# Moving the key-by-receptance products of a delta-rule recurrence ahead of it, through DRAM, and reordering one layer's projections

## Chip, cores, metric

One core of one Trainium2 chip runs the whole program. The metric is device time in microseconds (us) of that core. The kernel before has a median of 1447.89 us over 3 runs (1444.70 to 1640.55).

## What is computed

Two layers run over 1152 tokens (1024 of a prompt, 8 samples of 16) with 1024 features. Each layer normalises x, projects it to 24 features of 128 outputs, computes four branches from these, gates them, and projects the result back:

```python
z = rms_norm(x, p['norm_g']) @ p['w_in']
ya, shift_n, wkv_n = rwkv7_mix(za, shift0, s0, p)     # A: delta rule, per-token scan
yb, ckv, kr = mla_prompt(zb, p)                       # B: latent attention
yd, pool_n = pool_mix(zd, None, p)                    # D: trailing means of 2, 4, 8, 16 tokens
yc, vn = sgu_mix(zc, p)                               # C: spatial gating
y = jnp.concatenate([ya, yb, yc, yd], axis=-1) * jax.nn.silu(gates)
out = x + y @ p['w_out']
```

Branch A, for every token and each of 4 heads of 64, is

```python
sa = einsum('bhij,bhj->bhi', s, -kk_t)
s = s * w_t + outer(sa, kk_t * a_t) + outer(v_t, k_t)
y_t = einsum('bhij,bhj->bhi', s, r_t)
```

Branch C normalises its values over their 256 channels (`layer_norm`), mixes them over 128 positions and multiplies by u.

## The kernel before

Tokens are cut into 3 groups of 384. `project` makes one feature: 24 matmuls a group (8 slices of x, each as high by high, high by low and low by high part) into one of two PSUM buffers (`pj`), then a sink function that takes the result over. Weights come in quarter features: one DMA on SP (L238, three buffers), the high part on ACT (L241), the low part on POOL (L242), eight buffers each.

After chosen slices of a group, and after each sink, `project` calls `tick()`, which steps each open generator (a "lane") once. What TensorE does besides the projection is so laid between its matmuls, by hand, in program order. `inproj` sets the slices: (2, 5) gives 3 ticks a group, (1, 3, 5) gives 4. The order of the features is `F_ORDER`: WDAD and K0 together, K1, R0, R1, V0, V1 (keys, receptances, values of branch A), D0, GD0, D1, GD1 (pooling and its gates), VC0, VC1 (values of branch C), U0, GC0, U1, GC1 (its gating), and then attention.

Branch A works on 18 chunks of 64 tokens (16 prompt chunks, and 16 and 17 with the samples). `a_elem` (lane "a", once per key half and group) makes the decayed keys `kb` and the decayed negative keys and receptances `ar`. `systems` makes for each chunk the 64x64 products of keys (4 matmuls of 64x64 into `b`, a mask on DVE into `ns`, L514, two buffers) and writes them to DRAM (`nd`, L515, issued on ACT), two chunks per tick. `solve` loads all these systems, inverts 16x16 (samples) and 32x32 blocks with DVE alone (L538 a product, L540 an addition, 15 and 31 steps), copies (L550) and writes the inverses to DRAM (`dd`, L552 and L553, issued on ACT). `recurrence` then runs chunk by chunk, three ticks a chunk, in the order 16, 17, 0, ..., 15: `prepare` loads the inverse `tt` (L571, SP), makes the full products of keys with keys and receptances `gm` (4 matmuls of 64x128, two DVE masks of 128x256, L580), transposes keys and values (L586, L588); `advance` carries the state on.

`solve` is queued behind K1's systems, and `recurrence` is queued after D0, so that its first chunk comes in GD0. `pool_in` (D0, D1) takes windows with POOL and DVE (L784, L791). `gating` runs VC0 and VC1, then `norms` in lane "v" beside U0: for each of 9 blocks of 128 tokens two transposes on TensorE into one of two `st` PSUM buffers (L848), DVE statistics (L850, L852) and scaling (L855), two POOL operations (L856, L857), into tiles that GC0 and GC1 read.

Of the kernel before, what the change touches and what calls it, by code (L numbers as in the profile page):

```python
# [20 lines left out]
NS, SL = 8, 16  # L21
# [27 lines left out]
def tile_trunk(ctx: ExitStack, tc: tile.TileContext, *aps):  # L49
# [295 lines left out]
    for l in range(L):  # L345
# [14 lines left out]
        def inproj(f, sink):  # L360
            ticks = (3,)
            if f in (K1, R0, R1, V0, V1, D0, GD0, D1, GD1, VC0, VC1, GC0, U1, GC1,
                     GA0, GA1):
# [63 lines left out]
        def a_elem(i, g, k):  # L427
# [43 lines left out]
            V.scalar_tensor_tensor(out=kk, in0=k, scalar=vcol(V_KK + i), in1=q, op0=ALU.mult, op1=ALU.mult)  # L471
            V.scalar_tensor_tensor(out=ar[:, :, 0, :], in0=chv(kk), scalar=-1.0, in1=chv(ep),
                                   op0=ALU.mult, op1=ALU.mult)

            recip1p(av)
# [23 lines left out]


        nd, nds = halves(f"nd{l}", 32, 64), halves(f"nds{l}", 4, 64)

        def hp(h):
            return slice(64 * (h % 2), 64 * (h % 2) + 64)

        def systems(g):
            for cl in range(6):
                c = 6 * g + cl
                pn = pb()[:, 0:128].rearrange("p (i t) -> p i t", i=2)
                for h in range(4):  # L510
                    mm(pn[hp(h), h // 2, :], KB[h // 2][g][hp(h), cl, h % 2, :], AR[h // 2][g][hp(h), cl, 0, :])
                ns = chp.tile([128, 2, 64], F32, tag="u0", name=nm("ns"), bufs=2)
                mk = cm[:, C_MP if c < 16 else C_MS, 0:64]
                V.tensor_tensor(out=ns, in0=pn, in1=mk.unsqueeze(1).broadcast_to([128, 2, 64]), op=ALU.mult)  # L514
# [45 lines left out]
        def prepare(c):  # L560
# [12 lines left out]
            Gm = chp.tile([128, 2, 2, 128], F32, tag="gm", name=nm("gm"), bufs=2)  # L573
            for hh in range(2):
                pg = pb()[:, 0:256].rearrange("p (i t) -> p i t", i=2)
                pr = slice(64 * hh, 64 * hh + 64)
                for i in range(2):
                    mm(pg[:, i, :], KB[i][g][pr, cl].rearrange("p a t -> p (a t)"),
                       AR[i][g][pr, cl].rearrange("p a t -> p (a t)"))
                V.tensor_tensor(out=Gm[:, hh], in0=pg,  # L580
                                in1=cm[:, C_MS if samp else C_MP, :].unsqueeze(1).broadcast_to([128, 2, 128]),
                                op=ALU.mult)

# [241 lines left out]

        def gating():
            sg = m_tile(1024)
            sgb = sg[:, 0:512].rearrange("p (a i t) -> p a i t", a=2, i=2)
            SY.dma_start(out=sgb, in_=sgub[l])
            sgg = sg[:, 512:1024].rearrange("p (a t) -> p a t", a=2)  # L830
            SY.dma_start(out=sgg, in_=sgugb[l])
            vraw = []
            for fv in (VC0, VC1):
# [5 lines left out]
                vraw.append(vr)  # L839
            vn = [m_tile(1024), m_tile(1024), m_tile(1024)]  # L840

            def vnt(j):
                return vn[j // 4][:, (j % 4) * 256:(j % 4 + 1) * 256]

            def normalise(j):
                ps = st()[:, 0:256]
                for i in range(2):
                    PE.transpose(ps[:, i * 128:(i + 1) * 128], vraw[i][:, j * 128:(j + 1) * 128], ident)  # L848
                bs = smp.tile([128, 6], F32, tag="bs", name=nm("bs"))
                V.bn_stats(out=bs, in_=ps)  # L850
                mv = smp.tile([128, 2], F32, tag="mv", name=nm("mv"))
                V.bn_aggr(out=mv, in_=bs)  # L852
                rs = smp.tile([128, 1], F32, tag="rs1", name=nm("rs1"))
                rsqrt(rs, mv[:, 1:2], 1.0, ELN)
                V.tensor_scalar(out=vnt(j), in0=ps, scalar1=mv[:, 0:1], scalar2=rs, op0=ALU.subtract, op1=ALU.mult)  # L855
                Po.tensor_tensor(out=vnt(j), in0=vnt(j), in1=sgg[:, 0], op=ALU.mult)  # L856
                Po.tensor_tensor(out=vnt(j), in0=vnt(j), in1=sgg[:, 1], op=ALU.add)  # L857

            def norms():
                for j in range(9):  # L860
                    normalise(j)
                    if j % 2:
                        yield
                A.dma_start(out=vn_o[l], in_=vnt(8))
            go("v", norms())
            wst = m_tile(1024).rearrange("p (a h t) -> p a h t", a=2, h=4)
            SY.dma_start(out=wst[:, 0], in_=wsT[l])
# [6 lines left out]
            for i, (fu, fg) in enumerate(((U0, GC0), (U1, GC1))):  # L874
# [4 lines left out]
                inproj(fu, sink_u)  # L879
                finish("v")  # L880

# [23 lines left out]
        def after_k1(g, zs):  # L905
            start("a", a_elem(1, g, zs))
            if g > 0:
                go("a", systems(g - 1))
# [12 lines left out]
        values(V1)  # L921
        A.dma_start(out=shift_o[l], in_=sho)
        pool_in(0, D0)
        go("a", recurrence())
# [678 lines left out]
```

## Time and profile before

| | |
|---|---|
| median of 3 runs | 1447.89 us (1444.70, 1447.89, 1640.55) |
| profiled execution | 1447.32 us |
| its span, first to last instruction | 1445.5 us |
| granted TensorE clock, mean | 0.986 |
| TensorE (PE) busy | 1358.6 us, 94% of the span |
| DVE, ACT, POOL busy | 786.8, 746.6, 465.2 us |
| DMA traffic | 97.40 MB, 67 GB/s mean |

A row of a group of instructions gives the line, the engine, the operation, what it writes and reads, shapes and count; then the busy time of all, the mean of one in ns, and the idle time of the engine just ahead of them with what ended it. A matrix product of float32 data stands in the trace as several records: the 72 matmuls of 64x64 a layer are 288 records over both layers. A window row gives the busy time of each engine in a stretch of the span. A timeline row gives start, duration, engine and instruction, and in square brackets the idle time that went before on that engine. "SPq" and "ACTq" rows are DMA issues.

The layer 0 stages start at 15.4 us (WDAD and K0), 68.5 (K1), 90.7 (R0), 113.4 (R1), 131.3 (V0), 144.8 (V1), 159.3 (D0), 173.3 (GD0), 210.3 (D1), 234.0 (GD1), 261.8 (VC0), 289.9 (VC1), 314.3 (U0), 348.0 (GC0), 366.5 (U1), 379.2 (GC1) and 394.6 us (attention); those of layer 1 at 782.0 (K1), 871.3 (D0), 922.1 (D1), 1022.4 (U0) and 1055.2 us (GC0).

### The profile page before, as it was taken

Reading aid. Unit: us, or ns where it says so; the run is one execution under the profiler, and the core shown is the slowest. Engines: PE = TensorE matmul, PEld = TensorE weight load, DVE = VectorE, ACT = ScalarE, POOL = GpSimd, SP = SyncE. Lnnn points to the kernel's source line nnn. Section 1 sums busy time; section 2 is a strip of 40 time slices with the busy share of each in tenths; the row PEclk is TensorE's granted clock in tenths of the full one; section 3 lists DMA queues with packets and bytes.
Section 4 is the critical chain, followed back from the end, with each engine's and each line's share of the span. In section 5 each row is a group of like instructions: output and inputs, shape, how many; then the busy total and the mean of one; then the engine's idle time right before and its main releaser. Section 6 shows DMA issues by size and latency. Waiting matters only on the chain. (4 is left out here: it accounts for less than half of the span.)

```text
span 1445.5 us, 26910 instructions
## 1 busy us (share of the span) xinstructions
PE 1358.6 (94%) x9962; PEld 1160.2 (80%) x9962; DVE 786.8 (54%) x1766; ACT 746.6 (52%) x2013; POOL 465.2 (32%) x600
## 2 busy tenths in 40 slices
PE   4899989999999999999989998999999999899999
PEld 3768868888988886679977788788789788766998
DVE  6984954435235567742287948444532374777211
ACT  6762234655466677642257621555654676866210
POOL 4514404336411033332162234232653111322320
PEclk9799999999999999999999999999999999999999
DMA  7113241110312214033300122321022111131232
GB/s 222 52 32 75 63 102 42 61 49 25 96 46 70 60 37 128 5 116 93 99 22 30 49 64 66 92 69 49 29 71 74 52 57 59 45 103 45 74 95 77
DMA packets 116596, 97.40 MB, mean 67 GB/s; under 512 B 46129, under 2 KB 111345, under 8 KB 116465
## 3 DMA queue, kind: packets, MB, share of 16 engines
q1 hardware_dynamic: 76776, 73.74, 17.6%
q10 hardware_dynamic: 39688, 21.94, 5.1%
q8 instruction: 79, 1.29, 0.4%
q14 instruction: 53, 0.43, 0.1%
HBM read 71.48 MB, written 24.16 MB: 66 GB/s over the span
## 5 line engine op out<-in xcount | busy, mean ns | idle before, releaser
L76 PE MATMUL pj<-xh,wh 128*128 128x384 f32 x1152 | 415.4, 361 | 18.9 <-ACT xh L280 7.2
L76 PE MATMUL pj<-xl,wh 128*128 128x384 f32 x1152 | 396.4, 344 | 2.4 <-POOL xl L282 2.0
L76 PE MATMUL pj<-xh,wl 128*128 128x384 f32 x1152 | 396.3, 344 | 0.0
L242 POOL TENSOR_TENSOR wl<-wr,wh 128x256 fp32r<-128x256 f32 x200 | 157.0, 793 | 465.9 <-ACT wh L241 390.5
L76 PEld LDWEIGHTS pj<-xh,wh 128*128 128x128 f32 x1152 | 221.6, 193 | 41.7 <-ACT sho L400 11.3
L76 PEld LDWEIGHTS pj<-xl,wh 128*128 128x128 f32 x1152 | 222.1, 193 | 9.0 <-POOL xl L282 3.3
L76 PEld LDWEIGHTS pj<-xh,wl 128*128 128x128 f32 x1152 | 221.4, 192 | 6.0 <-issue 4.8
L76 PE MATMUL pj<-yh,wh 128*128 128x384 f32 x384 | 129.3, 337 | 2.4 <-DVE x L1426 2.4
L76 PE MATMUL pj<-yh,wl 128*128 128x384 f32 x384 | 128.6, 335 | 0.0
L76 PE MATMUL pj<-yl,wh 128*128 128x384 f32 x384 | 128.3, 334 | 0.0
L241 ACT ACTIVATE wh<-wr 128x256 fp32r<-128x256 f32 x200 | 81.0, 414 | 84.7 <-PE pj L76 41.0
L242 POOL TENSOR_TENSOR wl<-m,wh 128x256 fp32r<-128x256 f32 x56 | 43.7, 790 | 102.0 <-ACT wh L241 84.4
L76 PEld LDWEIGHTS pj<-yh,wh 128*128 128x128 f32 x384 | 72.1, 188 | 3.7 <-DVE x L1426 2.8
L76 PEld LDWEIGHTS pj<-yl,wh 128*128 128x128 f32 x384 | 72.1, 188 | 0.1
L76 PEld LDWEIGHTS pj<-yh,wl 128*128 128x128 f32 x384 | 72.1, 188 | 0.1
L1293 ACT ACTIVATE X<-b,ng 128x512 f32<-128x512 f32 (+3 forms) x96 | 55.0, 577 | 25.3 <-DVE ng L1285 21.4
L76 PE MATMUL b<-sp,cr 128*128 128x384 f32 (+3 forms) x192 | 59.5, 385 | 3.2 <-POOL sp L99 2.8
L1281 DVE TENSOR_REDUCE mx<-b 128x1 f32<-128x512 f32 (+3 forms) x96 | 53.0, 556 | 9.8 <-PE b L76 8.0
L1422 DVE TENSOR_TENSOR pt<-pj,pt 128x384 f32<-128x384 f32 x24 | 13.4, 557 | 80.6 <-PE pj L76 80.6
L76 PEld LDWEIGHTS st<-X,X 128*64 128x64 f32 x576 | 35.1, 136 | 27.4 <-ACT X L1311 7.6
L241 ACT ACTIVATE wh<-m 128x256 fp32r<-128x256 f32 x56 | 22.4, 413 | 61.0 <-PE pj L76 59.9
L1304 PE MATMUL pj<-cm,X 128*128 128x128 f32 x288 | 48.0, 286 | 5.0 <-ACT X L1293 5.0
(307 smaller groups left out, 2591.7 us busy)
## 6 DMA issues: line engine op xcount, KB each, us to landing
wr<-in_win_dram SPq DMA_DIRECT2D x176, 128.0 KB
m<-in_wout_dram SPq DMA_DIRECT2D x12, 512.0 KB
x<-in_xT_dram SPq DMA_DIRECT2D x12, 384.0 KB
ysp<-m ACTq DMA_DIRECT2D x24, 192.0 KB
pt<-in_xT_dram SPq DMA_DIRECT2D x24, 192.0 KB
ea<-ysp SPq DMA_DIRECT2D x24, 192.0 KB
x1d<-x ACTq DMA_DIRECT2D x24, 192.0 KB
pt<-x1d SPq DMA_DIRECT2D x24, 192.0 KB
```

Source lines behind the costliest of these rows:

```text
L76: return PE.matmul(out, lhsT=lhsT, rhs=rhs, start=start, stop=stop, skip_group_check=True)
L241: A.activation(out=h, in_=r, func=AF.Copy)
L242: Po.tensor_tensor(out=lo, in0=r, in1=h.bitcast(F32), op=ALU.subtract)
L1281: V.tensor_reduce(out=mx[:, b:b + 1], in_=pc[:, :w], axis=AX.X, op=ALU.max)
L1293: A.activation(out=P[:, :w], in_=pc[:, :w], func=AF.Exp, scale=SCALE, bias=ng, accum_out=sums[pr][:, b, s, h:h + 1])
L1304: PE.transpose(ptp[:, j * 128:(j + 1) * 128], Pb[slot][:, j * 128:(j + 1) * 128], ident)
L1422: V.tensor_tensor(out=xr, in0=ps, in1=xr, op=ALU.add)
```

## The change

The order of features becomes WDAD, K0, V0, R0, K1, R1, V1, VC0, VC1, D0, GD0, D1, GD1, U0, and on as before. `systems` makes the full products `gm` at once, one chunk per tick, from the second receptance's sink on, and stores with three SP DMAs per chunk: the key part into `nd` (two halves) and the whole tile, 256 KB, into a new DRAM tensor `gd`. `prepare` loads `gm` from `gd`. `a_elem` loses a subtraction and an exponential and uses the exponentials of the token before; one scaling moves from DVE to ACT. The gating values VC0, VC1 come ahead of the pooling, their norms run beside D0 and go to DRAM (`vnd`) and back. D1 and GD1 get 4 ticks a group in place of 3.

```diff
-F_ORDER = (WDAD, K0, K1, R0, R1, V0, V1, D0, GD0, D1, GD1, VC0, VC1, U0, GC0, U1, GC1,
+F_ORDER = (WDAD, K0, V0, R0, K1, R1, V1, VC0, VC1, D0, GD0, D1, GD1, U0, GC0, U1, GC1,
...
-            elif f in (U0, GB0, GB1):
+            elif f in (D1, GD1, U0, GB0, GB1):
                 ticks = (1, 3, 5)
...
-            V.tensor_tensor(out=rw, in0=cs, in1=rw, op=ALU.subtract)
-            ep = rw
-            A.activation(out=ep, in_=rw, func=AF.Exp, scale=-DECAY_C)
...
-            V.scalar_tensor_tensor(out=ar[:, :, 0, :], in0=chv(kk), scalar=-1.0, in1=chv(ep),
+            V.scalar_tensor_tensor(out=ar[:, :, 0, 1:], in0=chv(kk)[:, :, 1:], scalar=-1.0, in1=ex[:, :, 0:63],
                                    op0=ALU.mult, op1=ALU.mult)
+            V.tensor_scalar(out=ar[:, 0:nch, 0, 0], in0=chv(kk)[:, 0:nch, 0], scalar1=-1.0, scalar2=None, op0=ALU.mult)
...
-            V.tensor_scalar(out=av, in0=av, scalar1=vcol(V_KA + i), scalar2=nv[:, 11 + i:12 + i],
-                            op0=ALU.mult, op1=ALU.add)
+            A.activation(out=av, in_=av, func=AF.Identity, scale=vcol(V_KA + i), bias=nv[:, 11 + i:12 + i])
...
                 Po.tensor_tensor(out=ex, in0=chv(zs), in1=ex, op=ALU.mult)
+                if i == 1:
+                    go("a", systems(g))
...
-                pn = pb()[:, 0:128].rearrange("p (i t) -> p i t", i=2)
-                for h in range(4):
-                    mm(pn[hp(h), h // 2, :], KB[h // 2][g][hp(h), cl, h % 2, :], AR[h // 2][g][hp(h), cl, 0, :])
-                ns = chp.tile([128, 2, 64], F32, tag="u0", name=nm("ns"), bufs=2)
...
-                A.dma_start(out=whole(nd, c, 64) if c < 16 else whole(nds, c - 16, 64),
-                            in_=ns.rearrange("p i t -> p (i t)"))
-                if cl % 2:
-                    yield
+                Gm = chp.tile([128, 2, 2, 128], F32, tag="gm", name=nm("gm"), bufs=2)
...
+                    for i in range(2):
+                        mm(pg[:, i, :], KB[i][g][pr, cl].rearrange("p a t -> p (a t)"),
+                           AR[i][g][pr, cl].rearrange("p a t -> p (a t)"))
+                    V.tensor_tensor(out=Gm[:, hh], in0=pg, in1=mk.unsqueeze(1).broadcast_to([128, 2, 128]),
+                                    op=ALU.mult)
+                for hh in range(2):
+                    half = nds[2 * (c - 16) + hh] if samp else nd[2 * c + hh]
+                    SY.dma_start(out=half[0:128 * 64].rearrange("(s i t) -> s i t", s=64, i=2),
+                                 in_=Gm[64 * hh:64 * hh + 64, hh, :, 0:64])
+                SY.dma_start(out=gd[c], in_=Gm.rearrange("p h i t -> p (h i t)"))
+                yield
...
             Gm = chp.tile([128, 2, 2, 128], F32, tag="gm", name=nm("gm"), bufs=2)
-            for hh in range(2):
...
+            SY.dma_start(out=Gm.rearrange("p h i t -> p (h i t)"), in_=gd[c])
...
+                t = s_tile("gn", 3, 256)
+                V.tensor_scalar(out=t, in0=ps, scalar1=mv[:, 0:1], scalar2=rs, op0=ALU.subtract, op1=ALU.mult)
+                Po.tensor_tensor(out=t, in0=t, in1=sgg[:, 0], op=ALU.mult)
+                Po.tensor_tensor(out=t, in0=t, in1=sgg[:, 1], op=ALU.add)
+                SY.dma_start(out=vnd[j], in_=t)
...
+        def gating():
+            finish("v")
...
+                SY.dma_start(out=vn[a][:, 0:256 * n].rearrange("p (j t) -> p j t", j=n),
+                             in_=vnd[4 * a:4 * a + n].rearrange("j p t -> p j t"))
...
-        shifted(K1, lambda g: zk1[:, gcols(g)], after_k1)
-        go("a", idle(4))
-        go("a", systems(2))
-        go("a", idle(4))
+        values(V0)
+        receptance(0, R0)
+        shifted(K1, lambda g: zk1[:, gcols(g)], after_k1)
+        receptance(1, R1)
         go("a", solve())
-        receptance(0, R0)
-        receptance(1, R1)
-        values(V0)
         values(V1)
         A.dma_start(out=shift_o[l], in_=sho)
+        gating_values()
         pool_in(0, D0)
         go("a", recurrence())
```

DVE beside D0 of layer 0, before: solve steps (L538, L540) with the pooling windows (L791) between them.

```order
L791 SCALAR_TENSOR_TENSOR m_1717<-pt_1747,pinv_t,m_1716 64x384
L538 TENSOR_TENSOR m_1395<-m_1394,m_1393 128x252
L791 SCALAR_TENSOR_TENSOR m_1717<-pt_1749,pinv_t,m_1716 64x384
L540 TENSOR_TENSOR m_1394<-m_1394,m_1395 128x18x14
L538 TENSOR_TENSOR m_1395<-m_1394,m_1393 128x247
```

The same place now: solve steps (L551, L553), at an earlier step of the inversion, with the norms' statistics (L851, L853) and scalings (L857) between them.

```order
L553 TENSOR_TENSOR m_1706<-m_1706,m_1707 128x7x25
L851 BN_STATS bs_2012<-st_2009 128x6
L551 TENSOR_TENSOR m_1707<-m_1706,m_1705 128x192
L853 BN_AGGR mv_2014<-bs_2012 128x2
L851 BN_STATS bs_2027<-st_2024 128x6
L553 TENSOR_TENSOR m_1706<-m_1706,m_1707 128x8x24
L857 TENSOR_SCALAR gn_2019<-st_2009,mv_2014,rs_398_2016 128x256
L551 TENSOR_TENSOR m_1707<-m_1706,m_1705 128x207
```

At the first norm the block size of a solve step is 7x25 there, that is step 7 of 31, where before the pooling began at step 17; two solve operations stand between one norm's scaling and the next one's.

SP's DMA issues beside the recurrence of layer 0, before (`wr` weights, `tt` inverses, `m` tables of the gating):

```order
L571 DMA tt_2305<-dd_291 128x1x256
L829 DMA m_2937<-in_sgub_dram 128x512
L831 DMA m_2937<-in_sgugb_dram 128x512
L571 DMA tt_2414<-dd_291 128x1x256
L238 DMA wr_2524<-in_win_dram 128x256
L571 DMA tt_2558<-dd_291 128x1x256
```

and now, near the end of GD1:

```order
L584 DMA tt_2668<-dd_291 128x1x256
L587 DMA gm_2670<-gd_314 128x512
L584 DMA tt_2770<-dd_291 128x1x256
L874 DMA m_3458<-in_sgub_dram 128x512
L587 DMA gm_2772<-gd_314 128x512
L879 DMA m_3460<-vnd_318 128x4x256
L879 DMA m_3462<-vnd_318 128x4x256
L584 DMA tt_2872<-dd_291 128x1x256
```

Each chunk's load of `tt` has a load of `gm` behind it, of twice its size, and the normalised values come back through the same queue.

SP beside R1 and V1 now, where it issued weights alone before:

```order
L238 DMA wr_1566<-in_win_dram 128x256
L528 DMA nd_79_312<-gm_1296 128x1x64 x2
L530 DMA gd_314<-gm_1296 128x512
L528 DMA nd_79_312<-gm_1321 128x1x64 x2
L530 DMA gd_314<-gm_1321 128x512
L238 DMA wr_1590<-in_win_dram 128x256
```

Two chunks' six stores, each of which waits for its chunk's masks, stand between two weight loads.

## Rows read from the trace of the kernel before

**Rows 1.** The page's first part: engine, busy time, share of the span, instructions.

```profile
PE 1358.6 (94%) x9962; PEld 1160.2 (80%) x9962; DVE 786.8 (54%) x1766; ACT 746.6 (52%) x2013; POOL 465.2 (32%) x600
```

**Rows 2.** Windows: length, busy time per engine, granted clock, DMA share, GB/s.

```profile
68.50:159.30 90.80, 84.62 (x526) 72.32 (x526) 64.18 (x158) 40.24 (x105) 28.09 (x40) 0.97 0.20 54
159.30:210.30 51.00, 43.01 (x384) 38.14 (x382) 38.65 (x87) 15.99 (x50) 15.70 (x23) 0.97 0.36 77
210.30:234.00 23.70, 23.70 (x293) 20.43 (x292) 9.59 (x20) 10.68 (x41) 12.21 (x17) 1.00 0.26 83
234.00:348.00 114.00, 107.83 (x1272) 91.92 (x1271) 50.54 (x121) 62.52 (x215) 45.78 (x57) 0.99 0.16 48
366.50:379.20 12.70, 12.70 (x75) 12.61 (x74) 1.74 (x4) 4.57 (x11) 6.56 (x10) 1.00 0.50 153
782.00:871.30 89.30, 82.50 (x527) 70.70 (x527) 64.85 (x160) 41.83 (x109) 28.25 (x40) 1.00 0.21 55
871.30:922.10 50.80, 44.07 (x385) 39.10 (x383) 38.47 (x83) 15.98 (x50) 15.76 (x23) 0.93 0.34 77
922.10:1055.20 133.10, 130.05 (x1564) 111.14 (x1562) 59.54 (x140) 72.95 (x256) 57.70 (x73) 1.00 0.18 55
```

**Rows 3.** TensorE's products of `kb` and `ar`, by form, both layers.

```profile
L76 PE MATMUL b<-ar,kb 64*128 64x128 f32 x288 | 27.9, 298 | 0.0
L76 PE MATMUL b<-ar,kb 64*64 64x64 f32 x288 | 15.3, 228 | 4.6 <-DVE ns L514 3.7 <-DVE kb L481 0.8
```

**Rows 4.** Timeline, R1 of layer 0: two issues of `nd`, and a mask's wait.

```profile
121.47 0.49 ACTq L515 DMA_DIRECT2D nd<-ns  x1
...
124.65 0.29 DVE L514 TENSOR_TENSOR ns<-b,cm 128x128 f32<-128x128 f32 x1 [1.55 <-DMA nd<-ns]
```

**Rows 5.** DVE's masks and two operations of `a_elem`, by form, both layers.

```profile
L580 DVE TENSOR_TENSOR gm<-b,cm 128x256 f32<-128x256 f32 x72 | 28.3, 418 | 6.2 <-PE b L76 6.1
L514 DVE TENSOR_TENSOR ns<-b,cm 128x128 f32<-128x128 f32 x36 | 10.4, 288 | 22.5 <-DMA nd<-ns 21.1 <-PE pj L76 1.3
L463 DVE TENSOR_TENSOR ea<-ea,ea 128x384 f32<-128x384 f32 x12 | 7.8, 653 | 0.3
L482 DVE TENSOR_SCALAR ea<-ea,vcs,nv 128x384 f32<-128x384 f32 x12 | 7.4, 617 | 0.2
```

**Rows 6.** The solve on DVE, layer 0, from 143 to 188 us.

```profile
L538 DVE TENSOR_TENSOR m<-m,m 128x31 f32<-128x31 f32 (+15 forms) x31 | 13.5, 435 | 0.8
L540 DVE TENSOR_TENSOR m<-m,m 128x31 f32<-128x31 f32 (+15 forms) x31 | 13.2, 424 | 0.8
L538 DVE TENSOR_TENSOR m<-m 32x15 f32<-32x15 f32 (+7 forms) x15 | 3.8, 251 | 1.3 <-POOL wl L242 0.9
L540 DVE TENSOR_TENSOR m<-m 32x15 f32<-32x15 f32 (+7 forms) x15 | 3.5, 232 | 0.4
```

**Rows 7.** The norms of the gating values by form, both layers.

```profile
L855 DVE TENSOR_SCALAR m<-st,mv,rs 128x256 f32<-128x256 f32 x18 | 9.3, 533 | 0.7 <-ACT rs L214 0.7
L850 DVE BATCH_NORM_STATS2 bs<-st 128x6 f32<-128x256 f32 x18 | 7.1, 424 | 1.3 <-PE st L848 1.0
L848 PE MATMUL st<-cm,m 128*128 128x128 f32 x36 | 6.8, 289 | 3.6 <-DVE m L855 3.6
L856 POOL TENSOR_TENSOR m<-m,m 128x256 f32<-128x256 f32 x18 | 13.7, 762 | 4.7 <-DVE m L855 3.9 <-DVE mv L852 0.7
```

**Rows 8.** Timeline, D0 of layer 0: solve steps and a POOL operation.

```profile
160.00 0.39 DVE L540 TENSOR_TENSOR m<-m,m 128x220 f32<-128x220 f32 x1
...
160.80 0.73 POOL L242 TENSOR_TENSOR wl<-wr,wh 128x256 fp32r<-128x256 f32 x1 [1.09 <-ACT wh L241]
...
160.86 0.94 DVE L540 TENSOR_TENSOR m<-m,m 128x231 f32<-128x231 f32 x1
```

**Rows 9.** Waits of TensorE in GD0 of layer 0: us, times, longest.

```profile
PE b L76 <- DVE gm L580: 3.2, 2, 3.0
PE b L76 <- DVE m L666: 1.5, 2, 1.3
PE b L76 <- ACT m L610: 1.4, 1, 1.4
```

**Rows 10.** Timeline, GD1 of layer 0: an issue of `tt` and its first use.

```profile
230.60 0.50 SPq L571 DMA_DIRECT2D tt<-dd  x1
...
237.81 0.42 PE L76 MATMUL b<-tt,gm 64*64 64x32 f32 x8 [1.58 <-DMA tt<-dd]
```

More of the change, by code (lines that the diff above doesn't have):

```diff
@@ L361, in inproj @@
             ticks = (3,)
-            if f in (K1, R0, R1, V0, V1, D0, GD0, D1, GD1, VC0, VC1, GC0, U1, GC1,
+            if f in (K1, R0, R1, V0, V1, D0, GD0, VC0, VC1, GC0, U1, GC1,
                      GA0, GA1):
                 ticks = (2, 5)
-            elif f in (U0, GB0, GB1):
+            elif f in (D1, GD1, U0, GB0, GB1):
                 ticks = (1, 3, 5)
@@ L471, in a_elem @@
             V.scalar_tensor_tensor(out=kk, in0=k, scalar=vcol(V_KK + i), in1=q, op0=ALU.mult, op1=ALU.mult)
-            V.scalar_tensor_tensor(out=ar[:, :, 0, :], in0=chv(kk), scalar=-1.0, in1=chv(ep),
+            V.scalar_tensor_tensor(out=ar[:, :, 0, 1:], in0=chv(kk)[:, :, 1:], scalar=-1.0, in1=ex[:, :, 0:63],
                                    op0=ALU.mult, op1=ALU.mult)
+            V.tensor_scalar(out=ar[:, 0:nch, 0, 0], in0=chv(kk)[:, 0:nch, 0], scalar1=-1.0, scalar2=None, op0=ALU.mult)
+            if n < G:
+                V.tensor_scalar(out=ar[:, nch:, 0, :].rearrange("p c (s t) -> p c s t", t=SL)[:, :, :, 0],
+                                in0=chv(kk)[:, nch:].rearrange("p c (s t) -> p c s t", t=SL)[:, :, :, 0],
+                                scalar1=-1.0, scalar2=None, op0=ALU.mult)
             recip1p(av)
@@ L501, in tile_trunk @@
         nd, nds = halves(f"nd{l}", 32, 64), halves(f"nds{l}", 4, 64)
+        gd = dr.tile([18, 128, 512], F32, tag=f"gd{l}", name=nm("gd"))
         def hp(h):
@@ L508, in systems @@
                 c = 6 * g + cl
-                pn = pb()[:, 0:128].rearrange("p (i t) -> p i t", i=2)
-                for h in range(4):
-                    mm(pn[hp(h), h // 2, :], KB[h // 2][g][hp(h), cl, h % 2, :], AR[h // 2][g][hp(h), cl, 0, :])
-                ns = chp.tile([128, 2, 64], F32, tag="u0", name=nm("ns"), bufs=2)
-                mk = cm[:, C_MP if c < 16 else C_MS, 0:64]
-                V.tensor_tensor(out=ns, in0=pn, in1=mk.unsqueeze(1).broadcast_to([128, 2, 64]), op=ALU.mult)
-                A.dma_start(out=whole(nd, c, 64) if c < 16 else whole(nds, c - 16, 64),
-                            in_=ns.rearrange("p i t -> p (i t)"))
-                if cl % 2:
-                    yield
+                samp = c >= 16
+                Gm = chp.tile([128, 2, 2, 128], F32, tag="gm", name=nm("gm"), bufs=2)
+                mk = cm[:, C_MS if samp else C_MP, :]
+                for hh in range(2):
+                    pg = pb()[:, 0:256].rearrange("p (i t) -> p i t", i=2)
+                    pr = slice(64 * hh, 64 * hh + 64)
+                    for i in range(2):
[3 more added lines that the diff above has]
+                                    op=ALU.mult)
+                for hh in range(2):
+                    half = nds[2 * (c - 16) + hh] if samp else nd[2 * c + hh]
[3 more added lines that the diff above has]
+                yield
         def solve():
@@ L573, in prepare @@
             Gm = chp.tile([128, 2, 2, 128], F32, tag="gm", name=nm("gm"), bufs=2)
-            for hh in range(2):
[L575 to L582, printed above, removed]
+            SY.dma_start(out=Gm.rearrange("p h i t -> p (h i t)"), in_=gd[c])
             pt = pb()
@@ L823, in pool_gate, with gating_values @@
             inproj(fg, sink_gd)
[L826 to L830, printed above, removed]
+        vnd = dr.tile([9, 128, 256], F32, tag=f"vnd{l}", name=nm("vnd"))
+        def gating_values():
+            sgg = m_tile(512).rearrange("p (a t) -> p a t", a=2)
             SY.dma_start(out=sgg, in_=sgugb[l])
@@ L854, in normalise @@
                 rsqrt(rs, mv[:, 1:2], 1.0, ELN)
-                V.tensor_scalar(out=vnt(j), in0=ps, scalar1=mv[:, 0:1], scalar2=rs, op0=ALU.subtract, op1=ALU.mult)
-                Po.tensor_tensor(out=vnt(j), in0=vnt(j), in1=sgg[:, 0], op=ALU.mult)
-                Po.tensor_tensor(out=vnt(j), in0=vnt(j), in1=sgg[:, 1], op=ALU.add)
+                t = s_tile("gn", 3, 256)
[3 more added lines that the diff above has]
+                SY.dma_start(out=vnd[j], in_=t)
+                if j == 8:
+                    SY.dma_start(out=vn_o[l], in_=t)
             def norms():
@@ L863, in norms, with vnt @@
                         yield
-                A.dma_start(out=vn_o[l], in_=vnt(8))
             go("v", norms())
+        def gating():
+            finish("v")
+            sgb = m_tile(512).rearrange("p (a i t) -> p a i t", a=2, i=2)
+            SY.dma_start(out=sgb, in_=sgub[l])
+            vn = []
+            for a in range(3):
+                n = min(4, 9 - 4 * a)
+                vn.append(m_tile(1024))
+                SY.dma_start(out=vn[a][:, 0:256 * n].rearrange("p (j t) -> p j t", j=n),
+                             in_=vnd[4 * a:4 * a + n].rearrange("j p t -> p j t"))
+            def vnt(j):
+                return vn[j // 4][:, (j % 4) * 256:(j % 4 + 1) * 256]
             wst = m_tile(1024).rearrange("p (a h t) -> p a h t", a=2, h=4)
```

6 lines of the change are left out of this document (removed).

## Prediction

> **What bounds the kernel now.** I read the page's first part, then windows by stage, then groups by form, and last waits and the timeline where a stage stands idle. TensorE is busy 1358.6 of 1445.5 us [rows 1], so time is gained in two ways: fewer matmul records, or less idle time in the stages that have some. A projection alone takes 12.7 us (the window from 366.50 [rows 2]); what a stage has above that is branch work laid between its matmuls, or idle time. The idle time in the part that the change touches is small and in known places [rows 2]: 6.2 us from K1 to V1 (90.80 less 84.62) and 6.8 in layer 1; 8.0 and 6.7 in D0 and GD0; nothing in D1; 6.2 and 3.1 from there to the end of U0. Other engines are far from full except DVE in D0 and GD0, where it works 38.65 of 51.0 us, almost all of it the solve: 13.5 + 13.2 + 3.8 + 3.5 = 34.0 us of it a layer [rows 6], one chain in which each operation needs the one before. GD0's largest wait, 3.0 us, ends with DVE's first `gm` mask, which stands on DVE behind that chain [rows 9]. So in D0 and GD0 the limit is DVE, elsewhere TensorE.
>
> **The small products.** 288 records with 15.3 us busy go [rows 3]; they lie on TensorE's path, in stages with hardly a gap. The 64x128 products (27.9 us) only move. Against it stand 9 more interruptions of the projection a layer (one chunk a tick in place of two). The gain is 15.3 us; at worst 8, if each of the 18 interruptions costs 0.4 us, about one product's 0.43 (15.3 over 36 chunks); at best 17, from 60 ns a record in R1. I take 15.3.
>
> **Keys to V1.** Idle now: 6.2 + 6.8 = 13.0 us. Of these 4.6 are TensorE's waits for `ns` and `kb` [rows 3], and `ns` itself waits 21.1 us on DVE for the landing of `nd` [rows 5]: two buffers, and 3.2 us from the issue at 121.47 to the mask at 124.65 that reuses its buffer [rows 4], so 1.6 us a chunk. Now two `gm` buffers wait for three DMAs each. With two more issues at some 0.25 us beyond the 3.2 the round is 3.7 us, 1.85 a chunk (an estimate). TensorE needs more: a tick's share of the projection, 12.7/9 = 1.41, and a chunk's products, 27.9/36 = 0.78, together 2.19. So the stores stay hidden by 0.3 us a chunk. What is queued behind them on SP are weights, loaded two features, some 25 us, ahead. `a_elem` loses 0.65 and 0.62 us on DVE and an exponential on ACT per call [rows 5], and gets one or two small operations; DVE is at 71% there (64.18 of 90.80), so I cost this at nothing by itself; it shortens the chain to the first chunk. As the keys have V0 and R0 beside them, I take 5 us of the 13.0 as gone in both layers together, with ends at 0 and 9.
>
> **D0 and GD0.** This is the part that loses. Until now each of the 9 norms' statistics and scaling, 0.42 + 0.53 and some 0.25 for the small ones [rows 7], stood beside U0, where DVE has room. Now they stand in D0, with two solve operations (0.435 + 0.424 [rows 6]) between one and the next, as DVE's order shows: 2.06 us a norm. TensorE would be ready for a norm each 1.1 us (two a tick: 1.41 for the projection and two times 0.38 for transposes [rows 7], halved). The transposes write one of two `st` buffers, which the scaling of the norm two back frees, and TensorE runs in order, so D0 stretches by 9 x (2.06 - 1.1) = 8.6, less some 2.6 that the two buffers and the first norm's start give: 6 us a layer. The solve ends later by 9 x 1.2 = 10.8 us of norms less what it waits for now; of this 6 is already in D0. Then GD0 meets `u0`'s addition, now what stands on DVE behind the solve in place of the `gm` mask: 4 us; the mask `m` (L666), 1 us; the first prompt chunk's inverse by DRAM, 2 us; and the sample states' load, behind nine norm stores on SP, 1 us. Together 14 us a layer, 28 in both. Before: 8.0 + 6.7, and 3.6 that the transposes wait in U0 [rows 7], 18.3. So about 10 us more. Ends: 0 (DVE's norms fill the gaps of the solve chain) and 20 (all 10.8 us of norms come on top, in each layer).
>
> A POOL operation beside the solve costs DVE something: an L540 that takes 0.39 us alone took 0.94 where it began 0.06 us after a weight operation of 0.73 us on POOL [rows 8]. The norms bring 18 POOL operations of 0.76 us a layer [rows 7] into D0. If half of them meet a solve step, that is 9 x 0.55 = 5 us a layer, 10 in both, which is inside the end of 20; if all do, 20 in both (rival E). I take none, since by DVE's order a norm's POOL operations can fall beside its own statistics, which read PSUM.
>
> The Trainium skill has a rule on this, on the page "SBUF — State Buffer", section "Who interferes with whom": a DVE instruction with both inputs in SBUF contends with a GpSimd instruction that reads SBUF, and whichever is second waits for the whole of the first. The trace agrees in the one case above (0.55 us lost of POOL's 0.73). By the rule all 18 operations would hold up a solve step or wait for one, which is rival E; by the row alone it is one case, and my sum stays.
>
> **The recurrence, D1 to GC1.** A chunk is three ticks. At 3 ticks a group a chunk's own work is (23.7 - 12.7)/3 = 3.7 us [rows 2]; without its `gm` products, 0.78, it is 2.9; with 12 ticks a feature in D1 and GD1 it has 12.7/4 = 3.2 us of projection beside it: 6.1 us a chunk where there were 7.9. Within that `tt` must come: one took 7.2 us from its issue to its first use, of which TensorE waited 1.6 [rows 10]; and `gm`, 256 KB, stands behind it, at the 306 GB/s that 153 GB/s at a share of 0.50 mean [rows 2] another 0.86 us. In the SP order `tt` and `gm` are issued a chunk ahead, so mostly they are in time; queued behind them are weights with their 25 us of room and the gating's tables, needed in GC0. The 36 masks that leave this part (half of 28.3 us a layer [rows 5]) also end their waits, 6.1 us in both layers. The recurrence ends within GC1, with 72 ticks for some 57. The idle time now, 6.2 and 3.1, holds such waits; I take that what goes and what comes cancel: 0, with ends at -4 and +16 (0.5 us for each of 32 prompt chunks).
>
> **Sum.** 1447.3 - 15.3 - 5 + 10 + 0 = 1437 us. The profiled execution took 1447.32, the median is 1447.89, so no correction is due between them. What can be told from no change in this kernel is about 2%, 29 us: 1418 and 1476.
>
> **Rivals.** *DVE does not gate D0 (B).* The solve's start, one stage earlier against D0, lets it be done by GD0's first chunk, and the norms hide in the gaps. For: DVE stands idle 12.35 us in D0 and GD0 now [rows 2]. Against: that the chain of the solve is serial and the norms sit in it by order. Then the 14.7 us of idle time and the norms' 3.6 go, 18, and with the better ends of the other two terms: 1447 - 17 - 5 - 18 = 1407.
>
> *The loads set the recurrence's pace (C).* `tt` and `gm` are not there when a chunk comes: with 7.2 us to the first use against a period of 6.1, each of 32 prompt chunks waits 1.1 us, 35 us: 1472; with `gm` in a row behind `tt`, 0.86 more, 1500. It decides from the point where a load takes longer than 6.1 us. For: the one row. Against: the same row has weights issued between; that `gm` has no consumer of its bytes before the chunk's first product. I price it at 1480: slower than before.
>
> *The stores set the pace of the products (D).* If the three stores take their buffers for 5.4 us, 2.7 a chunk, TensorE waits 0.5 us for each of 18 chunks, 9 a layer: 1455. It decides from 4.4 us a round; the measured 3.2 is for one small store.
>
> *The contention of DVE and POOL is full (E).* Each of the 18 operations a layer costs the solve's chain 0.55 us, 9.9 a layer, 20 in both: 1457. For: rows 8. Against: DVE also does windows and statistics there, which the operations can fall beside.
>
> **How the numbers follow.** My case 0.60, B 0.17, C 0.10, D 0.06, E 0.07. My case alone gives 1424 to 1452 (its ends not all at once). Faster by over 2%: most of B, 0.14, and 0.02 of mine. Slower by over 2%: the most of C, 0.08. Same: 0.76. The range reaches toward B and C: 1412 to 1465 leaves out two thirds of B, 0.11, and C's 0.09.
>
> **What would show it.** Right: 288 records of 64x64 with `kb` are gone; TensorE's idle time in D0 is 4 to 8 us a layer and ends with DVE's scaling of a norm; GD0 waits for DVE and then `dd`; K1 to VC0 have under 4 us idle a layer; `tt` and `gm` end under 5 us of waits in D1 to GC0. Wrong: D0 runs at 14 us (B); the chunks of D1 and GD1 wait for `tt` or `gm` over 0.5 us each (C); the masks wait for `nd` or `gd` and TensorE for them (D).

## The result: 1480.2 us, 2.4% slower

The changed kernel takes 1480.20 us in the median of 4 runs (1479.67 to 1485.40), the kernel before 1451.09 us in 4 runs beside it: a ratio of 1.0237, with a 95% interval of 1.0213 to 1.026. One of these four, 1640.55 us, is far above the others and does not count in the ratio; the median of the other three is 1447.89 us. The forecast was 1437 us with a range of 1412 to 1465, so the result lies outside it and on the other side of no change. The profiled execution took 1479.86 us, its span is 1478.1 us, the mean granted clock 0.971 in place of 0.986.

The first part of the page, to be held against [rows 1]:

```profile
PE 1360.3 (92%) x9674; PEld 1157.1 (78%) x9674; DVE 774.1 (52%) x1722; ACT 746.0 (50%) x2013; POOL 466.8 (32%) x600
```

There are 288 matmul records less, and yet TensorE is not less busy: what the records gave was lost again inside the busy time. The windows show where, by stage; the columns are those of [rows 2]. For each layer they are V0 to VC1, D0, GD0, D1 and GD1.

```profile
68.10:187.60 119.50, 116.16 (x672) 103.15 (x672) 65.46 (x165) 47.33 (x123) 32.88 (x46) 0.98 0.33 94
187.60:215.50 27.90, 18.51 (x95) 16.15 (x94) 26.77 (x63) 7.48 (x26) 17.60 (x24) 0.88 0.17 54
215.50:247.90 32.40, 24.64 (x225) 21.14 (x223) 19.85 (x46) 8.21 (x26) 10.03 (x15) 0.84 0.50 97
247.90:287.10 39.20, 30.17 (x390) 24.22 (x389) 12.96 (x23) 16.94 (x66) 13.79 (x20) 0.91 0.43 132
287.10:319.80 32.70, 29.21 (x362) 24.14 (x359) 12.63 (x27) 19.98 (x68) 14.40 (x19) 1.00 0.39 106
795.40:913.90 118.50, 114.60 (x672) 101.27 (x672) 66.17 (x162) 47.83 (x124) 33.72 (x46) 1.00 0.33 96
913.90:942.10 28.20, 19.15 (x95) 16.63 (x94) 27.06 (x65) 7.64 (x28) 17.90 (x25) 0.82 0.17 53
942.10:974.70 32.60, 24.85 (x224) 21.36 (x222) 19.49 (x44) 8.14 (x26) 9.71 (x14) 0.79 0.51 95
974.70:1014.80 40.10, 32.30 (x393) 26.08 (x389) 12.83 (x23) 17.00 (x66) 13.83 (x20) 0.87 0.43 134
1014.80:1047.10 32.30, 30.21 (x364) 24.87 (x363) 14.00 (x29) 21.17 (x70) 14.46 (x19) 1.00 0.38 107
```

Length less busy time is the idle time of TensorE. It is small from V0 to VC1 (3.3 and 3.9 us; from K1 to V1 it was 6.2 and 6.8 before), 9.4 and 9.1 in D0, 7.8 and 7.8 in GD0, 9.0 and 7.8 in D1. The last column but two is the granted clock as a share of the higher of its two levels (2.4 GHz; the lower is 1.2): 0.79 to 0.91 through D0, GD0 and D1 in both layers.

What TensorE waited for, over the whole span (us, times, longest):

```profile
PE st L849 <- DVE gn L857: 17.7, 14, 2.1
PE b L76 <- DMA m<-in_S_dram: 15.5, 2, 7.8
...
PE b L76 <- DMA tt<-dd: 5.1, 1, 5.1
...
PE b L76 <- DMA gm<-gd: 4.4, 5, 1.5
```

The first is the norms' transposes in D0, which wait for the scaling of the norm two back. The second is the load of the sample states in GD0. The third is the inverse of the first prompt chunk (in layer 1 the same wait, 4.1 us, stands as "issue"). The new loads of `gm` cost 4.4 us in all.

Summing over the records of both layers from K1 (now V0) to the end of GC1, each until it ends or the next begins, the change of 31.0 us is made of +28.9 us of idle time, -10.8 us of products, +8.7 us in the projection's matmuls, whose number is the same, and +4.2 us in the rest. Of the 8.7 us, 7.8 lie in D0, GD0 and D1, where the clock was lower; whether the 4.2 us are the clock too is not shown. The first of these two windows holds the wait for the states, the other the 5.9 us after it.

```profile
221.30:229.10 7.80, 0.06 (x1) 0.00 (x0) 6.42 (x14) 1.63 (x3) 3.74 (x6) 0.85 0.75 146
229.10:235.00 5.90, 5.89 (x85) 5.15 (x86) 2.98 (x11) 0.83 (x3) 0.00 (x0) 0.50 0.10 36
```

After 7.8 us with one matmul the granted clock is 0.50, the lower of the two levels, for the whole of the next stretch. Over the span the means of 0.971 and 0.986 come to 86 us at the lower level in place of 40 (1478.1 and 1445.5 us, times what each mean lacks of 1, times two).

DVE has the chain behind most of this. It started the solve 9.8 us ahead of D0, where it had been some 16, and ended it 50 us after D0's start, where it had been 29; layer 1 agrees:

```profile
177.77 0.16 DVE L551 TENSOR_TENSOR m<-m 32x15 f32<-32x15 f32 x1 [6.76 <-DMA m<-nds]
...
236.28 1.05 DVE L563 COPY m<-m 128x1024 f32<-128x1024 f32 x1
```

Its first 6.76 us of waiting are the way of the last systems through DRAM. The solve's result then goes by DRAM too, and the first prompt chunk had its inverse 16.7 us after the solve's copy ended at 237.33: four issues on ACT ended at 243.09, the load was issued at 247.76.

```profile
247.76 1.10 SPq L584 DMA_DIRECT2D tt<-dd  x2
...
254.00 0.64 PE L76 MATMUL b<-tt,gm 64*64 64x32 f32 x8 [5.15 <-DMA tt<-dd]
```

In D0 one norm looks like this on DVE,

```profile
205.94 0.41 DVE L553 TENSOR_TENSOR m<-m,m 128x256 f32<-128x256 f32 x1
206.27 0.17 DVE L853 BATCH_NORM_AGGREGATE mv<-bs 128x2 f32<-128x6 f32 x1
206.38 0.83 DVE L551 TENSOR_TENSOR m<-m,m 128x255 f32<-128x255 f32 x1
207.13 0.42 DVE L851 BATCH_NORM_STATS2 bs<-st 128x6 f32<-128x256 f32 x1
207.47 0.60 DVE L553 TENSOR_TENSOR m<-m,m 128x255 f32<-128x255 f32 x1
207.99 0.53 DVE L857 TENSOR_SCALAR gn<-st,mv,rs 128x256 f32<-128x256 f32 x1
```

and on POOL at the same time:

```profile
206.09 0.83 POOL L858 TENSOR_TENSOR gn<-gn,m 128x256 f32<-128x256 f32 x1 [0.82 <-DVE gn L857]
207.01 0.78 POOL L859 TENSOR_TENSOR gn<-gn,m 128x256 f32<-128x256 f32 x1
```

A solve step that takes 0.41 us alone takes 0.83 and 0.60 beside the norm's two POOL operations. From one L857 to the next it is 2.51 us (205.48 to 207.99), not 2.06; three solve steps stand in between, not two as the order before the change had it. Summed over the solve, though, its 62 long steps took 28.4 us, against 26.7 in [rows 6]: with the norms' POOL operations beside some of them the chain is longer by 1.7 us (2.2 in layer 1).

The norms also hold D0's own projection. The sink that takes over D0's first group (L807, on ACT) waits for the last norm's transposes, because its tile takes over a buffer that they read (inferred from the kernel's ring of buffers). The projection writes one of two `pj` buffers, so it stands until this sink has run, and the last four norms come in a row with no projection between them:

```profile
203.64 0.41 PE L849 MATMUL st<-cm,m 128*128 128x128 f32 x2 [1.88 <-DVE gn L857]
206.16 0.61 PE L849 MATMUL st<-cm,m 128*128 128x128 f32 x2 [2.11 <-DVE gn L857]
208.67 0.66 PE L849 MATMUL st<-cm,m 128*128 128x128 f32 x2 [1.90 <-DVE gn L857]
209.16 0.49 ACT L807 ACTIVATE m<-pj 128x384 f32<-128x384 f32 x1 [2.16 <-PE st L849]
209.70 0.69 PE L76 MATMUL pj<-xh,wh 128*128 128x384 f32 x1 [0.37 <-ACT m L807]
```

### The profile page after: what moved, and what is told of

The parts are those of the page before. It is cut to its first block, busy times and chain, and to the rows that moved or that the text cites. A ratio compares the mean times of both kernels' runs of the same rounds, so it can differ in the third digit from the quotient of the medians.

```text
span 1478.1 us, 26565 instructions
## 1 busy us (share of the span) xinstructions
PE 1360.3 (92%) x9674; PEld 1157.1 (78%) x9674; DVE 774.1 (52%) x1722; ACT 746.0 (50%) x2013; POOL 466.8 (32%) x600
## 4 chain that ended last, share of the span: by engine, by line
PE 65%; DVE 16%; DMA 6%; ACT 4%; POOL 3%; issue 3%; SPq 1%; ACTq 0%; DVEq 0%; POOLq 0%
PE pj L76 39%; PE b L76 13%; PE st L76 8%; PE pj L1318 3%; DVE ea L278 2%; DMA gd<-gm 2%; DVE m L551 2%; DVE m L553 2%; POOL pt L789 2%; DMA gm<-gd 1%; SPq L528 1%; DVE ea L170 1%; DVE gm L524 1%; DVE kb L489 1%; DMA m<-in_S_dram 1%
## 5 line engine op out<-in xcount | busy, mean ns | idle before, releaser
L76 PE MATMUL st<-X,X 128*64 128x128 f32 x576 | 52.9, 285 | 0.0
```

The lines of the kernel that those rows point to most:

```text
L76: return PE.matmul(out, lhsT=lhsT, rhs=rhs, start=start, stop=stop, skip_group_check=True)
```

## Experiments

Theory: from VC1 to GD0 DVE has more to do than TensorE has beside it, and the norms put into the solve's chain make TensorE wait for it, first in D0, then through the late solve in GD0 and D1, with a lowered clock behind every wait. Rivals: SP's queue order (the states' load behind the norm stores); the new loads in the recurrence; the early start of the recurrence alone. Each time is of one run, but for the last experiment; the kernel before gave 1443.7 to 1449.7 beside them, so a few us are within the noise. A forecast called missed lies outside its stated range.

**The states' load on ACT.**

```diff
-                SY.dma_start(out=St["Ss"], in_=S0[l])
+                A.dma_start(out=St["Ss"], in_=S0[l])
```

> The changed kernel with one edit: the sample states' load (512 KB) is issued on ACT, so it no longer stands on SP behind the nine norm stores. Theory 1 (DVE's chain sets the end of GD0: the solve with the norms in it ran until 236.5 us in layer 0): the 7.8 us wait for the states goes, but the first chunk's addition stands on DVE behind the solve's steps until about 231.8 us, so TensorE waits for that instead and only some 2.7 us a layer are won: 1474 us. Theory 2 (the order of SP's queue is what costs): the two waits of 7.8 and 7.7 us go whole: 1464 us.

1481.4 us. Both were missed: the load did not go out earlier. On SP it had gone out at 223.99 us; on ACT the queue was free from 222.47, and yet the load went out at 225.35, right behind the last norm's second POOL operation:

```profile
222.06 0.41 ACTq L815 DMA_DIRECT2D out_pools_o_dram<-zsm  x1
...
224.60 0.72 POOL L859 TENSOR_TENSOR gn<-gn,m 128x256 f32<-128x256 f32 x1
225.35 0.37 ACTq L579 DMA_DIRECT2D m<-in_S_dram  x1
```

Layer 1 has the same two ends, 950.90 and 950.93 us. The states' tile takes over the buffer of the norms' gains, which that operation reads last (inferred from the kernel's ring of buffers and the semaphore that the load waits for). With the load on SP the last norm was done at 223.10, so the queue and its stores cost at most 0.9 us there: the norms themselves held the load.

**Nine ticks of nothing ahead of the recurrence.**

```diff
+        go("a", idle(9))
         go("a", recurrence())
```

> The changed kernel with nine ticks of nothing ahead of the recurrence, so that its first chunk comes in D1 instead of GD0. Theory 1 (the first chunks come before the solve, its way through DRAM and the sample states are ready): the waits for the states (7.8) and for the first inverse (5.1 and 4.1) go, and with them some 2 us a layer of lowered clock: 1480 - 25 - 4 = 1451 us, D0's 9 us a layer stay. Rival (the loads of inverses and products set the pace of the recurrence): the chunks wait elsewhere instead, over 0.5 us each, and the time stays at 1470 or more.

1480.6 us: missed. The waits for states and inverse went, and others came in D0 to D1 of layer 1:

```profile
PE st L849 <- DVE gn L857: 9.0, 7, 2.1
PE pj L76 <- DVE pt L764: 7.9, 2, 4.3
PE b L76 <- DVE m L671: 3.9, 2, 2.4
```

The first row is D0's wait, which was there before; the other two are new. L764 in layer 1 waits 4.3 us behind windows and solve steps on DVE. Then it waits 3.6 us while DVE itself is idle, because ACT, which makes its operand, stands at its own four issues of the inverses:

```profile
967.37 0.52 ACT L763 ACTIVATE pt<-pt 128x384 f32<-128x384 f32 x1 [8.91 <-DMA dd<-m]
```

So neither the late states nor the early start was the limit alone: what came next waited for DVE, or for ACT behind the solve's end. The loads as pace-setter did not show.

**Without the norms' POOL operations** (L858, L859 deleted).

> The changed kernel without the norms' two POOL operations (the affine part of the normalisation of the gating values is left out, 18 operations a layer). Theory 1 with contention (a POOL operation beside a solve step doubles that step, 0.83 us in place of 0.41, once a norm): D0's wait falls from 9 to about 5 us a layer, the solve ends some 4 us earlier, the result is 1464 to 1470 us. Rival (the pace of the norms in D0 is DVE's own work, POOL adds nothing): the solve steps stay at 0.83 us and the time at 1478 to 1482 us.

1472.5 us, 2.5 above the range and far from the rival's. D0's idle time fell from 9.4 to 2.7 us (window 19.20 us, 16.50 busy; 2.9 in layer 1), more than expected. But this is not the contention alone. The scalings still come 2.38 us apart in the mean, where it was 2.48, and some solve steps still take 0.84 to 0.93 us, beside POOL's weight operations. Without the POOL operations the gains are not read, the tile of D0's first sink gets another buffer, and the sink waits for no norm:

```profile
194.04 0.49 ACT L807 ACTIVATE m<-pj 128x384 f32<-128x384 f32 x1 [0.19 <-PE pj L76]
```

So the projection goes on between the norms. The run takes away the contention and this order together, and how much of D0's wait each had it does not show; as the scalings come hardly any closer, the order has the larger part by what is seen here. From V0 to GC1 the idle time fell by 13.9 us in all, though D1's rose from 9.0 to 11.6; the time fell by 7.7 only, with a mean clock of 0.966 in place of 0.971.

**The norms from VC1's sinks on**, one per tick (each group's three queued by its own sink).

> The changed kernel with each group's three norms queued from VC1's own sink, one per tick, so that they run in VC1's second and third group and in D0's first, beside the short 32-partition steps of the solve. Theory 1 (TensorE waits in D0 because the norms stand between long solve steps): the wait in D0 falls from 9 to 2 us a layer with less than 2 us new in VC1; the states' load leaves SP earlier and its wait shrinks too, though the solve with the norms ends little earlier: 1455 to 1465 us. Rival (DVE is simply too full from VC1 to GD0): the waits move into VC1 and GD0 and the time stays at 1475 or more.

1470.1 us: missed, between the two. D0 and VC1 together have 5.4 us of idle time in place of 9.4, GD0 and D1 16.3 in place of 16.8.

**Without the norms.**

```diff
-                ps = st()[:, 0:256]
...
-                Po.tensor_tensor(out=t, in0=t, in1=sgg[:, 1], op=ALU.add)
+                t = vraw[0][:, 0:256]
```

> The changed kernel without the norms of the gating values (transposes, statistics, scaling and the two POOL operations are left out, 256 raw values are stored in their place; stores and loads stay). Theory (DVE has more to do from VC1 to GD0 than TensorE has beside it: solve 34 us, norms 11, contention 7, windows 7, and so TensorE waits in D0, GD0 and D1): D0's 9 us go, the solve ends some 14 to 18 us earlier after D0's start, the waits for the states and the first inverses fall under 6 us a layer together, the clock stays up: 1430 to 1442 us. Rival (queues and the new loads hold the recurrence's start): D0's 9 us go but GD0 and D1 keep theirs, 1458 to 1465 us.

1453.6 us: 26.6 us less, most of the loss, though short of the 1442 expected. Of the 26.6 us, 17.1 are idle time and 5.9 the transposes' own time, which the kernel before pays too (4.0), beside U0; so not all of it is a price of the new place. The solve ended 33.5 us after D0's start, as expected, still 5 later than before. D0 has no idle time left, GD0 6.7 and D1 9.7:

```profile
187.90:200.40 12.50, 12.50 (x74) 12.50 (x73) 11.75 (x25) 3.03 (x7) 6.50 (x11) 1.00 0.49 143
200.40:230.90 30.50, 23.79 (x229) 20.73 (x227) 23.20 (x55) 8.47 (x29) 5.92 (x9) 0.94 0.40 72
230.90:273.40 42.50, 32.77 (x389) 26.33 (x389) 13.47 (x24) 16.69 (x65) 14.66 (x21) 0.84 0.39 121
```

**Without the norms, and nine ticks later** (both edits above).

> Without the norms (as above, they are left out) and with nine ticks of nothing ahead of the recurrence. Theory: what is left of the loss without the norms (6.7 and 9.7 us of idle time in GD0 and D1, 6.4 and 9.4 in layer 1, and the clock that falls after it) is that the first chunks come before the solve's results; with the solve no longer stretched by the norms nine ticks are enough, and 8 to 10 us of idle time a layer and some 3 of clock go: 1426 to 1438 us. Rival (the waits move to the pooling gates, as nine ticks did with the norms in place): 1448 us or more.

1446.8 us, within the noise of the kernel before and not the 1426 to 1438 expected. The first wait of GD0 and D1 is again L764, 5.5 us, a pooling gate behind the solve. So even with the norms left out, which the kernel before has to make, the new order only breaks even, with 10.8 us of products and 5.8 us of idle time ahead of D0 gone.

**Half of the 32x32 inversion**, in both kernels, which takes the same steps off DVE (15 of 31 run, so the result is not the inverse):

```diff
-                for s in range(n - 1):
+                for s in range(15):
```

> The changed kernel with 15 of the 31 steps of the 32x32 inversion (the last 16 steps, some 13 us of DVE a layer, 16 where POOL operations lie beside them, are left out). Theory (DVE's chain from VC1 to GD0 is what TensorE waits for): 13 to 16 us a layer less on that chain take 9 to 14 us a layer off the waits in D0, GD0 and D1 and lift the clock: 1446 to 1458 us. Rival (the waits hang on queues, the new order and the loads): 1472 us or more.

> The kernel before with the same 16 steps left out. Theory: of its 8.0 and 6.7 us of idle time in D0 and GD0 the most goes, and not more, since there DVE's chain is nearly covered: 1434 to 1440 us. So the same 13 us of DVE work a layer are worth 10 us before the change and 22 to 34 after it. Rival: as much is won as after the change.

1460.7 and 1437.1 us: 19.5 us less after the change, 10.6 before it (against 1447.75, the median of 17 runs beside it, 1445.70 to 1452.60). The second is as expected, the first 2.7 short. By these two runs the same DVE steps are worth almost twice as much in the new order. GD0 then has 0.1 us of idle time and D1 3.3. D0 holds the rest, 15.1 us, the norms' wait still among it:

```profile
PE st L849 <- DVE gn L857: 6.5, 3, 2.7
PE pj L76 <- ACT m L807: 5.8, 1, 5.8
PE st L849 <- DVE mv L853: 2.7, 1, 2.7
...
213.95 0.49 ACT L807 ACTIVATE m<-pj 128x384 f32<-128x384 f32 x1 [8.23 <-DMA dd<-m]
```

The 5.8 us come from the edit: the shorter solve ends within D0, and its four issues then hold ACT, and D0's sink with it (the last row). Without this the 19.5 us would rather be more.

**The products made again in the recurrence**, with neither store nor load of `gd`.

> The changed kernel with the products made a second time in the recurrence, as before the change, and neither stored whole nor loaded. Theory: the loads of the products cost only what the trace shows, 4.4 us of waits in both layers, and the products cost TensorE some 5.4 us a layer, with their masks on DVE: 1484 to 1492 us. Rival (loads of 256 KB a chunk set the pace of the recurrence): the time falls below 1475 us.

1502.7 us: 22.5 us more, 11 above the range. The products are now made whole twice: 576 records of 64x128, 28.2 us more of TensorE's time, while its idle time fell by 9.8 us. So loading the products is cheaper than making them again, and the loads do not hold the recurrence. What the change gains by this part the run does not price, since before it the first set was of 64x64 products, 13.5 us.

**VC0 and VC1 behind the pooling again**, norms beside U0, recurrence 19 ticks later.

> The changed kernel with VC0 and VC1 behind the pooling again, the norms beside U0, and the recurrence 19 ticks later. Theory: the norms' wait in D0 and the waits for states and first inverses go; the solve, which now runs from D0 to D1, makes the pooling gates wait on DVE by some 5 to 10 us a layer; 1440 to 1455 us. Rival (the place of the norms does not matter, the waits only move): 1470 us or more.

1469.8 us: missed by 15, and at the rival's 1470. In layer 0 the solve ran from 23 to 73 us after D0's start, so that it lay in GD0, D1 and GD1, and the pooling gates waited there:

```profile
PE pj L76 <- DVE pt L764: 11.0, 3, 6.5
```

**Cheaper norms.** The scaling on ACT, the two POOL operations late on the values read back, norms from VC1's sinks; then with six ticks of nothing; then with two chunks a tick.

```diff
-                V.tensor_scalar(out=t, in0=ps, scalar1=mv[:, 0:1], scalar2=rs, op0=ALU.subtract, op1=ALU.mult)
+                A.activation(out=t, in_=ps, func=AF.Identity, scale=rs, bias=nb)
```

> The norms from VC1's sinks on (as in the run above), scaled by ACT in place of DVE (0.53 us a norm off DVE), and the two POOL operations made late, on the values read back beside U0, so that none lies beside the solve. Theory (DVE's load from VC1 to GD0 decides, contention with it): against the version with the norms from VC1 (1470 us) the solve ends 10 to 12 us earlier, 4 to 6 us a layer of idle time go and some clock: 1452 to 1462 us. Rival (DVE's load is not the limit): 1466 us or more.

> The same with six ticks of nothing ahead of the recurrence. Theory: the waits of the first chunks (inverse by DRAM, first addition, sample mask) go, 5 to 8 us a layer and some 2 of clock: 1436 to 1448 us. Rival (they move into the pooling gates): within 4 us of the run without the six ticks.

> The same with two chunks of products per tick, as before the change, and four ticks of nothing ahead of the recurrence. Theory: the systems end 8 ticks, some 14 us, earlier, the solve has VC0 and VC1 whole beside it and is done about when the recurrence starts: 1425 to 1440 us. Rival (the stores, 3.7 us a round of two buffers, hold TensorE at two chunks a tick): masks wait for nd and gd, TensorE waits over 5 us a layer in R1 and V1, and little is gained over one chunk a tick.

1472.6, 1453.8 and 1457.3 us: all three were missed. The first is no gain over 1470.1. The six ticks then took 18.8 us, where nine had taken nothing from the changed kernel: with the scaling and the POOL operations out of the solve's way, the wait for the first chunks was worth its time. This is 26 us below the changed kernel, but not below the one before. Two chunks a tick brought the solve only 2.6 us further ahead of D0: there were two buffers. Twice the buffers and eight ticks:

> The version with cheap norms and two chunks a tick, with twice the buffers for the products (every second chunk in two half tiles of buffers that are free then), so that the systems end a group of the projection earlier, and with eight ticks of nothing ahead of the recurrence. Theory (what is left of the loss is that the solve starts late and runs into GD0 and D1): the solve starts 5 us or more earlier against D0's start, GD0 and D1 lose most of their 10 to 14 us a layer of idle time: 1430 to 1445 us. Rival (the recurrence itself, with its loads and DVE work beside 4 ticks a group, costs this time wherever it starts): 1452 us or more.

1480.9 us: missed. The solve did start earlier, 19.1 and 21.6 us ahead of D0, and the idle time of GD0 and D1 together fell only from 12.1 and 10.1 us a layer to 10.1 and 9.3. In GD1 this version has a fault of its own: an issue on ACT waits for the late POOL operations on 1024 columns, the recurrence's operations on ACT stand behind it for 8 us, and TensorE waits for these. GD1's idle time is 3.6 us a layer above that of the version before it, so this is the smaller part of the 23.6 us between the two; R1, VC1 and GC1 are each 3 to 5 us a layer longer, and why was not followed.

```profile
1005.89 0.34 ACT L720 ACTIVATE ar<-b 128x64 f32<-128x64 f32 x2 [8.05 <-POOL m L890]
```

So whether a still earlier solve would pay stays open.

**The shorter key chain alone**, in the kernel before; then also the norms scaled by ACT (no part of the change), in 12 runs.

> The kernel before with one part of the change: the shorter element-wise chain of the keys (no subtraction, one exponential less, one scaling on ACT). Theory: of the 6.2 and 6.8 us of idle time from K1 to V1 at most a third goes: 1443 to 1448 us, no difference that can be told. Rival (this chain is what the front gained from): 1438 us or less.

> The kernel before with the shorter element-wise chain of the keys and the norms scaled by ACT, measured in five rounds: the one look gave 1445.0 against 1449.7 us. Theory: 0.2 to 0.5% faster, by the front's idle time. Rival: no difference.

The first gave 1442.3 us beside 1443.7, a little below its range. The second had given 1445.0 beside 1449.7 in a run of its own, where 1438 to 1443 had been forecast; in 12 runs its median is 1445.75, beside 1447.75 in 17 runs of the kernel before, a ratio of 0.9988 with an interval of 0.9974 to 1.0002. No difference can be told, in either. No version tried that computes the whole result is clearly faster than the kernel before.

## Why the prediction was wrong

- **Small products**, -15.3 forecast: the 288 records went, but what the products gave back is 10.8 us. From each record to the next the 64x64 ones took 13.5 us; the other 1.8 of the 15.3 in [rows 3] lay over other records. And the 64x128 ones, which only move, take 2.8 us more where they now stand. Mis-sized by 4.5.
- **Keys to V1**, -5 forecast: 13.0 us of idle time became 7.2, so -5.8. Right. Here DVE waited 35.8 us for stores of `gm` in all, and TensorE 1.9 for DVE: the stores were hidden, rival D did not come.
- **D0 and GD0**, "together 14 us a layer": 17.2 and 16.8 were measured, and the parts were wrong. D0 cost 9.4 and 9.1 in place of 6: a norm takes 2.51 us and not 2.06, since three solve steps stand between two scalings, not two, and two of them meet a POOL operation, which the sum took as none; and D0's sink, which the sum did not see, waits for the last norm. The states' load cost 7.8 in place of 1: it goes out when the last norm is done with a buffer, and not by its place behind the stores. That the solve starts 6 us later against D0 had no term either; rival B even has it one stage earlier.
- **D1 to GC1**, "0": this is the step that failed most, though the stated end of +16 still holds what came. 14.4 and 11.0 us of idle time, against 6.6 and 3.5 before (the transposes' 3.6 us in U0 among these), so +15. The sum let the solve's delay end in GD0, with 2 us for the first prompt chunk's inverse by DRAM. But the solve ended 50 us after D0's start, its result took 16.7 us more, and the first prompt chunk stood waiting for it: 5.1 and 4.1 us of the 15. The rest is smaller waits, such as the recurrence's operations on DVE behind pooling windows. No run put D1 and GD1 back to 3 ticks a group, so what the faster pace has in this is not shown.
- **The clock** had no term. The waits in a row brought it to 0.79 to 0.91 in three stages of each layer, and the projection alone lost 8.7 us.

In one sentence: the prediction saw that DVE's chain was the limit of D0 and GD0 and that the norms were put into it, but priced only the first wait that this causes. Taking the norms out gave 26.6 us, of which 17.1 are waits; taking half the inversion out gave almost twice as much as before, by single runs. Rival C had almost the time, 1480, by another mechanism: `gm` and `tt` waits were some 14 us, not the 35 and more that it counts, 9 of them for the first prompt chunk alone, and doing without the loads made the kernel slower. Rival E had the cause of the slower steps, but its 0.55 us for each of 18 operations is too much: over the whole solve its steps took 1.7 and 2.2 us more a layer than before.

What stays open: what is left of GD0's and D1's waits without the norms comes, where it was followed, from the late solve (the pooling gate behind it), but no version with an earlier solve ran without a new fault of its own, so it is not shown that an earlier one would take them away.

On the rule of the Trainium skill ("SBUF — State Buffer", "Who interferes with whom") that a DVE instruction with two inputs in SBUF contends with a GpSimd instruction that reads SBUF, the trace agrees: 0.83 in place of 0.41 us for a step that starts 0.3 us into a POOL operation of 0.83.

## What to carry over

Before moving work next to a serial chain on a shared engine, add up that engine's whole load up to the chain's last consumer against what TensorE has beside it; what does not fit is paid at each later place that needs the chain, not once. Give each row of waits a term for the clock. And a wait named in a profile is worth its time only if nothing behind it waits for the same chain: moving the recurrence's start away by nine ticks changed the names of the waits and not the time, and six ticks gave 19 us once the norms' scaling and POOL operations were off that chain. Where an engine waits for another one's last use of a buffer, look which tile had the buffer before: the states' load and D0's sink both waited for the norms in that way, and neither the queue nor the engine named beside them was the reason.

## What was not expected of the hardware

An idle stretch of 7.8 us was followed by 5.9 us at half clock, so a wait of TensorE cost more than its length. An operation on ACT can stand 6 to 9 us behind that engine's own four DMA issues of the inverses (8.2 and 8.9 us in the rows above), long enough to hold TensorE by way of a sink.
